# Half 2's best-entry tiles: from diagonal products on TensorE to sums on VectorE, ScalarE and GpSimd; low-part products at the end of a weight

## The chip, the cores and the metric

The kernel runs on one core of a Trainium2 chip. The metric is the device time of one execution in microseconds (us), and of several executions the median. The core has five engines that work through queues of their own, in order, and wait for each other by semaphores: TensorE (in the profile PE, its weight loads PEld), VectorE (DVE), ScalarE (ACT), GpSimd (POOL) and SyncE (SP). DMAs are issued from the queues of SP, ACT and POOL, and 16 DMA engines carry them.

## What is computed

One layer of a decoder on 1024 tokens of width 1024, in float32. First a mixer: a gated linear attention and a chunked gated MLP side by side, merged and projected. Then an expert mixer (PEER), which is where most of the change lies. A token has 8 heads; each head picks its 16 best of 16384 single-neuron experts by two half keys, and the layer sums the experts' outputs:

```python
def peer(h, w_q, keys1, keys2, expert_down, expert_up):
    q = jnp.einsum('btd,dq->btq', h, w_q).reshape(B, T, H, 2, PEER_DQ // 2)
    s1 = jnp.einsum('bthc,kc->bthk', q[..., 0, :], keys1)
    s2 = jnp.einsum('bthc,kc->bthk', q[..., 1, :], keys2)
    v1, i1 = lax.top_k(s1, K)
    v2, i2 = lax.top_k(s2, K)
    ...
    top_s, pos = lax.top_k(cand, K)
    idx = jnp.take_along_axis(cidx, pos, axis=-1)
    g = jax.nn.softmax(top_s, axis=-1)
    def block(args):
        xx, ii, gg = args
        u = expert_down[ii]
        a = jax.nn.gelu(jnp.einsum('pd,ped->pe', xx, u), approximate=False)
        vv = expert_up[ii]
        return jnp.einsum('pe,ped->pd', gg * a, vv)
```

The inputs are drawn so that the scores are far apart: a head's best expert nearly always carries weight, and of the others only a few do. The kernel uses that. Each token's best expert of each head is a "direct entry"; the others, where their gate isn't negligible, are packed into dense lists ("sorted entries"), and a few heads that need more are redone as "rare" rows.

## The kernel before

**Halves and blocks.** The tokens are worked in two halves of 512 (variable `hf`), each of four blocks of 128 tokens: blocks 0 to 3 are half 1, blocks 4 to 7 half 2 (`BH` is 4, the first block of half 2).

**Weight streams.** All large products go through `stream` (L1145): for each of 8 steps k it loads a 128x512 piece of a weight (`wt`, from SP's queue), ACT rounds it to the high part `wh` (L1156), and POOL or DVE takes the rest as the low part `wl` (L1158). `body` then issues for each of four PSUM tiles three products, high by high, high by low and low by high, in `mm3` (L178; products at L179, L180 and L181). `feat` tells the feature-major groups (the weight is stationary: q and k, and the query weights) from the token-major ones (the weight is moving); in the first, `lh` and `ll` are the weight's parts, in the second `rh` and `rl`. So the low part of the weight is used in the third product at L181 of feature-major groups and in the second at L180 of token-major ones. `group` (L1165) is a stream of one weight, `w_out_part` (L1450) one of two, and `w_q` (L1485) is the query projection, whose first weight is streamed in two half-width passes with a body of its own, the other three through `group`. Four buffers each hold `wt`, `wh` and `wl`.

**The expert work beside it.** After each step k, `step` (L945) pumps side queues, generators that emit a little work each time. `direct_rows` (L675) does the direct entries of half 1 while half 2's mixer runs: it gathers an expert's two rows for 128 tokens, forms the dot product on DVE and adds the weighted row to a tile `yd` in SBUF, mostly with DVE (L715), for head 4 with ACT (L712) and POOL (L713). `peer_stream` (L721) does everything else, starting behind half 2's linear attention and going on beyond the last weight. Its list `todo` holds pairs (block, j): j from 0 to 7 are direct entries, one per head, j from 8 to 17 the sorted entries, and 18 (`last`) adds the rare rows and finishes the block. While weights are still streamed, its entries use small buffers (`pl["own"]` is False) and 0.84 to 1.3 pumps a step; behind the last weight it gets its own buffers and a second accumulator (`own` True), and all engines. Entries are listed 2 ahead in the first case (their gathers are issued from POOL's queue, L487), 7 ahead in the second. Each entry takes two pumps.

**A direct entry of half 2.** `direct_list` gathers `uv` (128 tokens by 2048: the expert's input row and its output row, 1 MB); `direct_dot` forms the dot product with `h2l` on DVE (L497), the GELU and the gate on ACT (L499, L500), and a diagonal matrix `Wd` of the weights, also on ACT (L502). `add_rows` (L560) lets PE multiply `Wd` with the output row into the accumulator `acc` in PSUM (L564; two products of 512 columns, in float32). When a run of entries ends, `rows_keep` (L604) copies `acc` to a tile `yb` in SBUF (`kept[b]`, ACT, L609), or adds it to the one that is there (DVE, L606). `rare_rows` (L577) later multiplies `yb` with the modulation row (POOL, L589) and adds it to the block's residual (L590).

**The order.** `EARLY` and `LATER` list the runs of half 2's direct entries. Before the end of the weights (`stage1`) come: 6 rare entries of half 1, blocks 0 to 3, then (5, heads 0 to 3), (6, 0 to 3), (7, 0 to 5) and block 4's heads 0 to 5, whose accumulator stays open. Then come (5, 4 to 7), (6, 4 to 7), (7, 6 and 7), block 4's last two heads with its ten sorted entries, six rare entries, and the rest of blocks 5 to 7. `load_h2` (L460) loads `h2l` once a run, from ACT's queue. Where the weights end before the list up to `stage1` is through, the rest of it is done behind them. The order in which an engine's queue finally holds its instructions is chosen by a planner that places the program's instructions by their order and by durations of its own (`schedule_with_timeline_sim`, L1631), so an instruction can stand ahead of others that the program names first.

## Time and profile before

| | us |
|---|---|
| median of 3 runs (1611.24 to 1613.67) | 1613.54 |
| the profiled execution | 1611.35 |
| its span, from the first instruction to the last | 1609.3 |
| PE / DVE / POOL / ACT busy in it | 1421.2 / 1093.7 / 833.4 / 772.6 |
| POOL: low parts of weights, 257 of 368 | 374.1 |
| DVE: low parts of weights, 111 of 368 | 105.0 |
| ACT: high parts of weights, 368 | 227.2 |
| sorted entries: expert products on PE in the second stage (184 records) | 91.0 |

The profile is one execution as the hardware profiler saw it. A row of a group reads: line, engine, operation, out<-in, shapes, count | busy time in us, mean duration in ns | idle time of the engine just before, and what ended it. One float32 product of the direct entries shows as two records. A busy PE isn't a PE at its peak, since products overlap: one of 128x512 with rounded operands lasts 0.39 us and the next starts 0.23 us behind it. The rows that the argument needs are in the prediction.

### The profile page before, as it was taken

The numbers are of one execution on the slowest core, as the hardware profiler recorded it, in microseconds if no ns is written. First come the engines' busy times: TensorE is split into PE (matmuls) and PEld (weight loads), VectorE is DVE, ScalarE is ACT, GpSimd is POOL, SyncE is SP. The second block draws the span as 40 slices with busy tenths as digits, with TensorE's granted clock in tenths as the row PEclk, the third lists the DMA queues.
The fourth block names the chain that finished last, engine by engine and source line by source line (L and its number), as shares of the span: only waits on it lengthen the run. The fifth ranks groups of instructions, "written<-read, shape, count | busy, mean of one in ns | idle before, by whom it ended". The sixth has DMA issues, their size and how long they took to land.

```text
span 1609.3 us, 20188 instructions
## 1 busy us (share of the span) xinstructions
PE 1421.2 (88%) x6076; PEld 1067.0 (66%) x6076; DVE 1093.7 (68%) x2777; ACT 772.6 (48%) x1677; POOL 833.4 (52%) x682
## 2 busy tenths in 40 slices
PE   5999989999998998898988889998879997778984
PEld 3777757888777786576766667876658764345542
DVE  7664654111446698977788787878787875787782
ACT  4554333332446454745445566556555553445541
POOL 5331247643275455645666688555666563434331
PEclk7999989999999999899999999999999999989998
DMA  9643633224377556737856787956777778978972
GB/s 318 231 143 112 190 125 112 92 85 137 100 247 255 173 167 219 271 99 249 293 181 206 258 302 262 367 190 209 274 268 263 251 275 316 368 293 316 393 292 83
DMA packets 123335, 361.48 MB, mean 225 GB/s; under 512 B 16761, under 2 KB 27257, under 8 KB 107346
## 3 DMA queue, kind: packets, MB, share of 16 engines
q0 software_dynamic: 30336, 175.39, 29.4%
q1 hardware_dynamic: 70272, 132.15, 25.0%
q10 hardware_dynamic: 22610, 52.58, 9.3%
q8 instruction: 49, 0.80, 0.2%
q14 instruction: 68, 0.56, 0.1%
HBM read 335.22 MB, written 24.85 MB: 224 GB/s over the span
## 4 chain that ended last, share of the span: by engine, by line
PE 47%; DVE 21%; DMA 14%; issue 7%; ACT 6%; POOL 4%; ACTq 0%; SPq 0%; DVEq 0%; POOLq 0%
PE mm L180 10%; PE mm L181 10%; PE mm L179 10%; PE acc L564 7%; DMA wada<-in_w_ada_dram 3%; DMA uv<-in_tab_dram,ix 3%; DVE vl L573 2%; DMA uv<-in_tab_dram,dix 2%; DVE uv L542 2%; PE hps L540 2%; DVE wl L1158 1%; DMA uvd<-in_up_dram,dix 1%; PE hps L541 1%; DMA uvd<-in_down_dram,dix 1%; POOL wl L1158 1%
## 5 line engine op out<-in xcount | busy, mean ns | idle before, releaser
L1158 POOL TENSOR_TENSOR wl<-wt,wh 128x512 fp32r<-128x512 f32 x257 | 374.1, 1461 | 355.8 <-ACT wh L1156 320.3
L180 PE MATMUL mm<-wl,hTh 128*128 128x512 f32 x896 | 367.4, 410 | 10.0 <-DVE wl L1158 5.1
L179 PE MATMUL mm<-wh,hTh 128*128 128x512 f32 x896 | 342.7, 412 | 27.2 <-ACT wh L1156 7.7
L1156 ACT ACTIVATE wh<-wt 128x512 fp32r<-128x512 f32 x368 | 227.2, 626 | 281.4 <-PE mm L181 163.8
L181 PE MATMUL mm<-wh,hTl 128*128 128x512 f32 x896 | 361.2, 406 | 0.2 <-DVE hTl L1115 0.2
L179 PEld LDWEIGHTS mm<-wh,hTh 128*128 128x128 f32 x896 | 173.1, 194 | 79.0 <-ACT wh L1156 12.2
L1158 DVE TENSOR_TENSOR wl<-wt,wh 128x512 fp32r<-128x512 f32 x111 | 105.0, 946 | 159.8 <-ACT wh L1156 155.4
L180 PEld LDWEIGHTS mm<-wl,hTh 128*128 128x128 f32 x896 | 173.6, 194 | 56.8 <-POOL wl L1158 9.2
L181 PEld LDWEIGHTS mm<-wh,hTl 128*128 128x128 f32 x896 | 173.4, 194 | 41.7 <-issue 1.3
L179 PE MATMUL mm<-hTh,wh 128*128 128x512 f32 (+1 forms) x448 | 168.1, 377 | 10.5 <-ACT vt L1203 5.3
L487 POOL DMA_INDIRECT uv<-in_tab_dram,ix x92 | 98.5, 1070 | 150.5 <-PE tps L511 35.2
L180 PE MATMUL mm<-hTl,wh 128*128 128x512 f32 (+1 forms) x448 | 164.3, 368 | 0.0
L181 PE MATMUL mm<-hTh,wl 128*128 128x512 f32 (+1 forms) x448 | 159.8, 370 | 1.3 <-DVE wl L1158 0.9
L542 DVE SCALAR_TENSOR_TENSOR uv<-uv,hps 128x512 f32<-128x512 f32 x144 | 95.0, 682 | 38.3 <-PE hps L541 21.0
L573 DVE SCALAR_TENSOR_TENSOR vl<-uv,r,vh 128x512 fp32r<-128x512 f32 x92 | 89.1, 999 | 37.9 <-ACT vh L572 37.9
L179 PEld LDWEIGHTS mm<-hTh,wh 128*128 128x128 f32 x448 | 86.1, 193 | 26.9 <-ACT vt L1203 7.7
L181 PEld LDWEIGHTS mm<-hTh,wl 128*128 128x128 f32 x448 | 85.3, 192 | 16.3 <-DVE wl L1158 1.5
L180 PEld LDWEIGHTS mm<-hTl,wh 128*128 128x128 f32 x448 | 86.2, 192 | 14.0 <-issue 0.7
L564 PE MATMUL acc<-uv,W 128*128 128x512 f32 x184 | 91.0, 618 | 1.4 <-ACT W L557 1.2
L564 PE MATMUL acc<-uv,Wd 128*128 128x512 f32 x128 | 66.0, 655 | 28.1 <-ACT Wd L502 24.3
L540 PE MATMUL hps<-hh,E 128*128 128x512 f32 x144 | 72.3, 508 | 14.4 <-DVE uv L542 7.1
L564 PEld LDWEIGHTS acc<-uv,Wd 128*128 128x128 f32 x128 | 24.9, 206 | 58.4 <-ACT Wd L502 33.6
(958 smaller groups left out, 2662.3 us busy)
## 6 DMA issues: line engine op xcount, KB each, us to landing
wt<-in_w_inp_dram SPq DMA_DIRECT2D x224, 256.0 KB, 3.0
wt<-in_w_qp_dram SPq DMA_DIRECT2D x80, 256.0 KB, 3.2
wada<-in_w_ada_dram SPq DMA_DIRECT2D x32, 512.0 KB, 4.5
wt<-in_w_outp_dram SPq DMA_DIRECT2D x64, 256.0 KB, 3.1
wada<-in_w_ada_dram SPq DMA_DIRECT2D x32, 256.0 KB, 6.0
s_d<-so ACTq DMA_DIRECT2D x32, 256.0 KB, 3.2
h2l<-h_d ACTq DMA_DIRECT2D x13, 512.0 KB, 7.3
xr<-in_x_dram ACTq DMA_DIRECT2D x8, 512.0 KB, 4.1
```

The source lines that it names most:

```text
L179: nc.tensor.matmul(ps, lh, rh, start=first, stop=False)
L180: nc.tensor.matmul(ps, lh, rl, start=False, stop=False)
L181: return nc.tensor.matmul(ps, ll, rh, start=False, stop=last).ins
L487: nc.gpsimd.indirect_dma_start(out=uv[:], out_offset=None, in_=tab, in_offset=bass.IndirectOffsetOnAxis(ap=ix, axis=0))
L540: nc.tensor.matmul(hps, Ej, hh[:, sl], start=True, stop=False)
L541: nc.tensor.matmul(hps, Ej, hl[:, sl], start=False, stop=True)
L542: nc.vector.scalar_tensor_tensor(uv[:, sl], uv[:, sl], 1.0, hps, op0=OP.mult, op1=OP.mult, accum_out=r[:, 2 + n:3 + n])
L564: nc.tensor.matmul(acc[:, sl], W, v[:, sl], start=first, stop=last)
L573: nc.vector.scalar_tensor_tensor(vl, v, r[:, 5:6], vh.bitcast(F32), op0=OP.mult, op1=OP.subtract)
L1156: nc.scalar.activation(wh, wt, AF.Identity)
L1158: eng.tensor_tensor(wl, wt, wh.bitcast(F32), op=OP.subtract)
```

## The change

Two things are changed.

1. `mm3s` replaces the calls of `mm3` in `group` and in `w_out_part`. In steps 1 to 6 of a stream it issues, for all four PSUM tiles, the two products that don't need the weight's low part, and then the four that do. In steps 0 and 7 the order is the old one. Query weight 0, with its two half-width passes, keeps `mm3`.

2. The direct entries of half 2 are no longer multiplied by a diagonal on PE. `direct_dot` gives the weight column and the output row to `direct_sum`: the first entry of a block creates `kept[b]` on ACT, the others are added to it, with `own` and an even head by DVE in one operation, else by ACT (scaling the row in place) and POOL (the add). `rows_keep` is left with the add. A run of direct entries opens no accumulator. The lists change: heads 4 and 5 of blocks 5 and 6 come in the first list in the place of block 4's heads 0 to 5, and block 4's eight heads are the last run of the second list, just ahead of its sorted entries.

```diff
-EARLY = ((5, 0, 4), (6, 0, 4), (7, 0, 6))
-LATER = ((5, 4, 8), (6, 4, 8), (7, 6, 8))
+EARLY = ((5, 0, 4), (6, 0, 4), (7, 0, 6), (5, 4, 6), (6, 4, 6))
+LATER = ((5, 6, 8), (6, 6, 8), (7, 6, 8), (4, 0, 8))
...
+    def mm3s(sets, k):
+        if k in (0, KD - 1):
+            for ps, lh, ll, rh, rl, feat in sets:
+                mm3(ps, lh, ll, rh, rl, k == 0, k == KD - 1)
+            return
+        for ps, lh, ll, rh, rl, feat in sets:
+            nc.tensor.matmul(ps, lh, rh, start=False, stop=False)
+            nc.tensor.matmul(ps, *((lh, rl) if feat else (ll, rh)), start=False, stop=False)
+        for ps, lh, ll, rh, rl, feat in sets:
+            nc.tensor.matmul(ps, *((ll, rh) if feat else (lh, rl)), start=False, stop=False)
...
-        W = pl["pq"].tile([P, P], F32, name="Wd", tag="W", bufs=3 if pl["own"] else 2)
-        nc.scalar.activation(W, ident, AF.Identity, scale=r[:, 2:3])
-        yield W, uv[:, D:]
+        yield r[:, 2:3], uv[:, D:]
+
+    def direct_sum(pl, b, j, wv):
+        w, v = wv
+        if b not in kept:
+            kept[b] = rowp.tile([P, D], F32, name="yb", tag="row") if b > BH else pl["ph"].tile([P, D], F32, name="yb")
+            nc.scalar.activation(kept[b], v, AF.Identity, scale=w)
+        elif pl["own"] and j % 2 == 0:
+            nc.vector.scalar_tensor_tensor(kept[b], v, w, kept[b], op0=OP.mult, op1=OP.add)
+        else:
+            nc.scalar.activation(v, v, AF.Identity, scale=w)
+            nc.gpsimd.tensor_tensor(kept[b], kept[b], v, op=OP.add)
...
     def rows_keep(pl, b, acc):
-        if b in kept:
-            nc.vector.tensor_tensor(kept[b], kept[b], acc, op=OP.add)
-            return
-        kept[b] = rowp.tile([P, D], F32, name="yb", tag="row") if b > BH else pl["ph"].tile([P, D], F32, name="yb")
-        nc.scalar.activation(kept[b], acc, AF.Identity)
+        nc.vector.tensor_tensor(kept[b], kept[b], acc, op=OP.add)
...
+        def direct(b, j0, j1):
+            runs.add((b, j0))
+            todo.extend((b, j) for j in range(j0, j1))
+
         rows = range(PH, last + 1)
         seg(NBLK, range(PH, PH + NTR[0]))
         for b in range(BH):
-            seg(b, range(0 if b not in summed else PH, last + 1))
-        for b, j0, j1 in EARLY:
-            seg(b, range(j0, j1))
-        seg(BH, range(6), close=False)
+            seg(b, rows)
+        for run_ in EARLY:
+            direct(*run_)
         stage1 = len(todo)
-        for b, j0, j1 in LATER:
-            seg(b, range(j0, j1))
-        seg(BH, range(6, last), open_=False)
+        for run_ in LATER:
+            direct(*run_)
+        seg(BH, range(PH, last))
...
             nw = weights(nw, nd)
+            if j < PH:
+                direct_sum(use[-1], b, j, wvs.pop(k))
+                del ents[k]
+                yield
+                continue
...
-                    for i in range(4):
-                        cs = slice(i * P, (i + 1) * P)
-                        if feat:
-                            mm3(pss[i], wh[:, cs], wl[:, cs], hTh[:, k], hTl[:, k], k == 0, k == KD - 1)
-                        else:
-                            mm3(pss[i], hTh[:, k, cs], hTl[:, k, cs], wh, wl, k == 0, k == KD - 1)
+                    cuts = [slice(i * P, (i + 1) * P) for i in range(4)]
+                    if feat:
+                        mm3s([(pss[i], wh[:, cs], wl[:, cs], hTh[:, k], hTl[:, k], True) for i, cs in enumerate(cuts)], k)
+                    else:
+                        mm3s([(pss[i], hTh[:, k, cs], hTl[:, k, cs], wh, wl, False) for i, cs in enumerate(cuts)], k)
...
-                    for m in range(4):
-                        cs = slice((2 * p + m // 2) * P, (2 * p + m // 2 + 1) * P)
-                        mm3(pss[m], hTh[:, k, cs], hTl[:, k, cs], ws[m % 2][0], ws[m % 2][1], k == 0, k == KD - 1)
+                    cuts = [slice((2 * p + m // 2) * P, (2 * p + m // 2 + 1) * P) for m in range(4)]
+                    mm3s([(pss[m], hTh[:, k, cs], hTl[:, k, cs], *ws[m % 2], False) for m, cs in enumerate(cuts)], k)
```

More of the change, by code (lines that the diff above doesn't have):

```diff
@@ L727, in seg @@
                 opens.add((b, js[0]))
-            if js[0] < PH:
-                runs.add((b, js[0]))
             todo.extend((b, j) for j in js)
```

## The prediction

> **What bounds the kernel now.** I read the page first (span, engines, chain), then the windows that cut the span where the direct entries of half 2 run, then the groups and the waits of those windows, and the timeline last.
>
> ```profile
> span 1609.3 us, 20188 instructions
> PE 1421.2 (88%) x6076; PEld 1067.0 (66%) x6076; DVE 1093.7 (68%) x2777; ACT 772.6 (48%) x1677; POOL 833.4 (52%) x682
> PE 47%; DVE 21%; DMA 14%; issue 7%; ACT 6%; POOL 4%; ACTq 0%; SPq 0%; DVEq 0%; POOLq 0%
> PE mm L180 10%; PE mm L181 10%; PE mm L179 10%; PE acc L564 7%; DMA wada<-in_w_ada_dram 3%; DMA uv<-in_tab_dram,ix 3%; DVE vl L573 2%; DMA uv<-in_tab_dram,dix 2%; DVE uv L542 2%; PE hps L540 2%; DVE wl L1158 1%; DMA uvd<-in_up_dram,dix 1%; PE hps L541 1%; DMA uvd<-in_down_dram,dix 1%; POOL wl L1158 1%
> ```
>
> TensorE holds most of the chain: the weight products L179 to L181 and, with 7%, the expert sums of L564. The direct entries touch only two stretches, so I cut the span there.
>
> ```profile
> core 0: us, PE busy (x) PEld busy (x) DVE busy (x) ACT busy (x) POOL busy (x), PEclk, DMA share, GB/s
> 0.00:1270.00 1270.00, 1148.79 (x5180) 907.40 (x5181) 855.87 (x1840) 622.30 (x1247) 699.97 (x563) 0.96 0.61 207
> 1270.00:1347.00 77.00, 72.68 (x309) 52.95 (x307) 53.22 (x221) 36.45 (x78) 43.20 (x40) 0.98 0.78 277
> 1347.00:1420.00 73.00, 48.12 (x116) 21.30 (x117) 56.27 (x216) 31.06 (x92) 30.51 (x27) 0.88 0.81 308
> 1420.00:1609.30 189.30, 151.65 (x474) 85.36 (x472) 128.35 (x502) 82.82 (x262) 59.76 (x55) 0.91 0.73 287
> ```
>
> From 1270 to 1347 (**stage A**, the last query weights with direct entries between them) PE is busy 72.7 of 77 us: it is the bound. From 1347 to 1420 (**stage B**, direct entries and the routing of half 2, no weights left) no engine fills the time: DVE has 56.3, the DMA engines 81%, PE 48. That stage is a chain through all of them. Behind 1420 no direct entry is left.
>
> ```profile
> L564 PE MATMUL acc<-uv,Wd 128*128 128x512 f32 x128 | 66.0, 655 | 28.1 <-ACT Wd L502 24.3 <-DVE yb L606 2.2 <-issue 1.4
> L564 PE MATMUL acc<-uv,Wd 128*128 128x512 f32 x40 | 19.8, 622 | 2.8 <-ACT Wd L502 2.8
> L564 PE MATMUL acc<-uv,Wd 128*128 128x512 f32 x85 | 45.0, 672 | 25.3 <-ACT Wd L502 21.5 <-DVE yb L606 2.2 <-issue 1.4
> ```
>
> These are the diagonal products: whole run, stage A, stage B (three records more lie on the edge). 128 records for 32 entries are four each, so 10 entries fall in stage A and 22 in stage B. The number of steps that an entry takes does not change, so I keep that split.
>
> **Part 1, low-part products last.** What it can win is the time that PE waits for a wl:
>
> ```profile
> PE mm L180 <- DVE wl L1158: 5.1, 2, 4.0
> PE mm L180 <- POOL wl L1158: 4.6, 7, 1.3
> PE mm L181 <- DVE wl L1158: 0.9, 1, 0.9
> PE mm L181 <- POOL wl L1158: 0.5, 1, 0.5
> ```
>
> That is 11.1 us in all, the ceiling. The first product with wl moves from second place (third in the feature-major groups) to ninth. The pace is the distance of two starts:
>
> ```profile
> 1275.73 0.39 PE L180 MATMUL mm<-hTl,wh 128*128 128x512 f32 x1
> 1275.96 0.39 PE L181 MATMUL mm<-hTh,wl 128*128 128x512 f32 x1
> ```
>
> 0.23 us, so a late wl gains 7 x 0.23 = 1.6 us. Of the wait of 4.0 us 1.6 go, of the other at L180 from DVE 1.1, of the seven from POOL all 4.6: 7.3. Steps 0 and 7 of a stream keep the old order; with 6 of 8 steps that is 5.5, and I take **-6**. No product is added; wh is free four products earlier. Bounds: 0 (a wh that is late instead) and -11.
>
> **Part 2, the sums leave PE.** The 32 entries become 4 that create kept[b] on ACT (the first of each block), 10 that DVE adds (even heads among the 22 of stage B), and 18 that ACT scales and POOL adds: 3 + 0 + 7 in stage A, 1 + 10 + 11 in stage B. Half 1 already does the same operations on the same shapes, and those rows give the prices:
>
> ```profile
> L715 DVE SCALAR_TENSOR_TENSOR yd<-uvd,rdr,yd 128x1024 f32<-128x1024 f32 x24 | 32.8, 1365 | 4.3 <-DMA uvd<-in_up_dram,dix 4.0
> L502 ACT ACTIVATE Wd<-ident,rd 128x128 f32<-128x128 f32 x32 | 12.8, 401 | 7.6 <-PE acc L564 6.5 <-ACT rd L500 0.4
> L713 POOL TENSOR_TENSOR yd<-yd,uvd 128x1024 f32<-128x1024 f32 x4 | 11.2, 2798 | 10.7 <-ACT uvd L712 10.7
> L708 ACT ACTIVATE yd<-uvd,rdr 128x1024 f32<-128x1024 f32 x4 | 4.6, 1149 | 1.3 <-DVE rdr L706 1.3
> L712 ACT ACTIVATE uvd<-uvd,rdr 128x1024 f32<-128x1024 f32 x4 | 4.6, 1142 | 4.1 <-DVE rdr L706 2.8 <-DMA uvd<-in_up_dram,dix 1.3
> L609 ACT ACTIVATE yb<-acc 128x1024 f32<-128x1024 f32 x4 | 4.1, 1020 | 2.9 <-PE acc L564 2.9
> L606 DVE TENSOR_TENSOR yb<-yb,acc 128x1024 f32<-128x1024 f32 x3 | 3.7, 1218 | 4.2 <-PE acc L564 4.2
> ```
>
> ACT loses 32 diagonals and four copies of an accumulator (12.8 + 4.1) and gains 18 x 1.14 and 4 x 1.15 (25.1 together): 8 us more on an engine that is busy 48% and waits in both stages, so I cost it at nothing. If it came late, the POOL add behind it would wait (rival D).
>
> Stage A. PE loses 19.8 us of products and the wait of 2.8: 22.6, down to 54.4. Who is late next?
>
> ```profile
> L487 POOL DMA_INDIRECT uv<-in_tab_dram,dix x16 | 17.6, 1100 | 18.0 <-PE mm L181 5.1 <-PE acc L564 4.9 <-PE aux L1537 3.7
> L1158 POOL TENSOR_TENSOR wl<-wt,wh 128x512 fp32r<-128x512 f32 x12 | 16.8, 1404 | 15.6 <-ACT wh L1156 11.6 <-DMA wt<-in_w_qp_dram 3.9
> L646 POOL TENSOR_TENSOR fin<-fin,fw 128x1024 f32<-128x1024 f32 x1 | 2.4, 2412 | 0.0
> L497 DVE SCALAR_TENSOR_TENSOR uv<-uv,h2l 128x1024 f32<-128x1024 f32 x11 | 16.0, 1453 | 16.1 <-DMA uv<-in_tab_dram,dix 13.9 <-issue 2.2
> L366 DVE COPY_PREDICATED v<-bits,v 128x448 f32<-128x448 uint32 (+3 forms) x8 | 9.3, 1163 | 0.0
> ```
>
> POOL has 43.2 us there (gathers, low parts, three steps of 2.4 like L646 for a finished block). Seven adds of 2.80 make 62.8: the stage cannot be shorter than that, a gain of 14. And POOL and DVE shut each other out:
>
> ```profile
> 1393.39 2.40 POOL L589 TENSOR_TENSOR yb<-yb,g2row 128x1024 f32<-128x1024 f32 x1 [0.22 <-DVE yb L606]
> 1404.80 3.26 POOL L589 TENSOR_TENSOR yb<-yb,g2row 128x1024 f32<-128x1024 f32 x1 [5.88 <-DVE yb L606]
> 1393.50 2.31 DVE L398 TENSOR_TENSOR qr<-qt,lane 128x1 f32<-128x1 f32 x1
> 1404.63 1.22 DVE L497 SCALAR_TENSOR_TENSOR uv<-uv,h2l 128x1024 f32<-128x1024 f32 x1
> ```
>
> An operation of DVE on one column took 2.31 us and ended with POOL's multiply, which had started just before it; POOL's next one started behind a DVE product and took 0.86 longer. If such pairs exclude each other wholly, stage A needs 16.0 + 9.3 (DVE) + 16.8 + 3 x 2.4 + 7 x 2.8 (POOL) = 68.9, a gain of 8. Between 8 and 14 I take **-10**; ends 0 and -22.6. The Trainium skill has this as a rule that speaks against the change: by "SBUF — State Buffer", section "Who interferes with whom", a VectorE instruction with two SBUF inputs and a GpSimd instruction that reads SBUF share one port pair, and the second blocks until the first has ended. By that rule, with which the four rows above agree, the gain is the 8 and not the 22.6.
>
> Stage B.
>
> ```profile
> L497 DVE SCALAR_TENSOR_TENSOR uv<-uv,h2l 128x1024 f32<-128x1024 f32 x21 | 25.1, 1215 | 4.7 <-DMA uv<-in_tab_dram,dix 4.7
> L589 POOL TENSOR_TENSOR yb<-yb,g2row 128x1024 f32<-128x1024 f32 x3 | 8.0, 2672 | 7.2 <-DVE yb L606 7.2
> POOL uv L487 <- PE acc L564: 9.8, 5, 5.0
> ```
>
> What goes: PE's 45.0 us, POOL's wait of 9.8 for gather buffers that PE frees, DVE's wait of 4.2 (L606) and its three adds of 3.7. What comes: DVE 10 x 1.37 = 13.7, so 66.3 of 73 in its queue; POOL 11 x 2.80 = 30.8, so 61.3. The DMA engines need 0.81 x 73 = 59 for the same rows. Without mutual blocking DVE's 66.3 would be the floor: -7. With it, 25.1 + 13.7 + 30.8 + 8.0 = 77.6: +5. The rows show the blocking, so I take **+4**. The first gather of block 4's sorted entries waits on the routing that is threaded through this DVE queue, so what the stage loses delays all that follows.
>
> Moved steps: block 4's entries leave stage A's list and four of blocks 5 and 6 take their place, with their gathers on POOL; the runs of one block become nine in place of eight, so one load of h2 more goes into ACT's queue.
>
> ```profile
> h2l<-h_d ACTq DMA_DIRECT2D x13, 512.0 KB, 7.3
> ```
>
> It is hidden while the seven entries gathered ahead are worked off; without that cover it costs 7.3. Two accumulators are free in stage B where block 4 held one, but nothing of that stage accumulates any more: nothing.
>
> **Sum.** -6 - 10 + 4 = -12. The profiled execution took 1611.35 us (span 1609.3 and 2 around it), so 1599.4; it lies 2.2 under the median of 1613.54, which becomes 1601.5.
>
> **Rivals.**
> - B, **all hides**: DVE, POOL and ACT overlap as they do in most of the span (68%, 52%, 48% busy) and PE's relief comes through: -8 - 20 - 7 = -35, 1578.5. For it: PE is the bound in stage A and most POOL idle time there was a wait on others. Against: the blocking rows.
> - C, **blocking takes it back**: POOL adds of 3.26, as in the row at 1404.80, make 72.1 in stage A (-5) and 82.7 in stage B (+10): -6 - 5 + 10 = -1, 1612.5. For it: those rows; against: half of DVE's work there (top-k, PSUM reads) need not collide. It is what the Trainium skill's rule above ("SBUF — State Buffer") would make of the time.
> - D, **POOL waits in its queue**: an add waits for the row that ACT scales, and behind it stand the gathers and low parts. L713 shows POOL idle 10.7 us before four adds, 2.7 each. In stage A 7 x (2.8 + 2.7) + 43.2 = 81.7 (+5), in stage B 11 x 5.5 + 30.5 = 91 (+18): 17 more with part 1, 1630.5. It decides from a wait of 1.1 us an add in stage B (30.5 + 11 x 3.9 = 73). Against: in half 1 an add had little else to follow; here the dot product runs an entry ahead.
> - That the reordering does nothing, because the wait moves to wh, is the zero end of part 1; it shifts every case by 6.
>
> **How the numbers follow.** A, the sum: 0.50 (own range 1592 to 1611). B 0.18, C 0.14, D 0.18. I forecast A, 1601.5. The range runs from 1577, inside B, to 1622, between C and D, which leaves about a tenth on each side. About 0.2% (3 us) is what a measurement can tell from no change: A and B are faster (0.68), C is the same (0.12 with the ends of its neighbours), the rest, D and a bad C, is slower (0.20).
>
> **What would show it.** Part 1: the waits for wl at L180 and L181 fall from 11.1 to about 5 and those for wh do not grow by it. Stage A: from the start of the third query group to the last key product some 10 us less, PE no longer at 94%, POOL's busy share over 85%. Stage B: as long as now or longer, with DVE near 90% busy, DVE operations on few columns that take over 2 us, POOL adds of 2.4 to 3.3. B is right if adds stay at 2.4 and stage B falls under 68 us; D if POOL idles over 1 us before an add for ACT. The sum is wrong from the start if the planner of the issue order places other work differently before 1270, where only part 1 acts.

## The result and the profile after

The changed kernel takes 1629.05 us, the median of 4 runs (1625.36 to 1636.17), beside 1612.79 for the kernel before, also of 4. The medians lie 16 us apart; the ratio taken from all these runs is 1.0107, 95% interval 1.0071 to 1.0144, which is 17 us. It is slower, where 12 us less were forecast. The profiled execution took 1627.85 us. From its page, engines and chain:

```profile
PE 1365.9 (84%) x5948; PEld 1048.7 (64%) x5948; DVE 1151.2 (71%) x2784; ACT 788.8 (49%) x1669; POOL 880.4 (54%) x701
DVE 18%; PE 17%; ACT 5%; issue 5%; DMA 4%; POOL 1%; ACTq 0%; SPq 0%; DVEq 0%; POOLq 0%
```

PE lost 55 us of work (1421.2 before), DVE gained 58 and POOL 47. The chain does not reach back over the whole span, so these shares aren't comparable with those of before one by one; but DVE now leads it.

To see where the time went I cut both spans at two events that both kernels have: the start of the last weight product, and the start of the first dot product of a sorted entry of half 2 (DVE, uv<-uv,hps). Windows of after, then of before; the columns are the window, its length, busy time of PE, PEld, DVE, ACT and POOL with counts, granted clock, DMA share, GB/s:

```profile
1270.00:1322.90 52.90, 43.58 (x198) 35.67 (x196) 40.76 (x175) 24.65 (x46) 42.20 (x31) 0.90 0.67 230
1322.90:1447.20 124.30, 16.57 (x65) 12.89 (x63) 117.79 (x338) 55.50 (x125) 76.74 (x56) 0.54 0.74 267
1447.20:1626.10 178.90, 145.25 (x454) 80.57 (x454) 123.54 (x420) 74.50 (x239) 60.71 (x53) 0.92 0.75 287
```

```profile
1270.00:1339.80 69.80, 66.99 (x284) 49.42 (x283) 50.75 (x217) 33.82 (x69) 38.64 (x36) 0.98 0.77 273
1339.80:1425.60 85.80, 57.31 (x157) 27.07 (x155) 62.98 (x257) 37.60 (x110) 38.54 (x33) 0.90 0.82 311
1425.60:1609.30 183.70, 148.15 (x458) 83.11 (x458) 124.11 (x465) 78.91 (x252) 56.28 (x51) 0.91 0.72 285
```

The weights end 16.9 us earlier, as meant. The sorted entries take 4.8 us less. But the stretch between, with the direct entries that come behind the weights, grew from 85.8 to 124.3 us: +38.5. (Below, "the stretch" is this one.) PE is nearly idle there, at half its clock, and DVE is busy 117.8 of 124.3 us, where it had 63.0 of 85.8. The groups of the stretch in the changed kernel:

```profile
L508 DVE SCALAR_TENSOR_TENSOR uv<-uv,h2l 128x1024 f32<-128x1024 f32 x25 | 34.4, 1406 | 1.0 <-DMA uv<-in_tab_dram,dix 1.0
L523 POOL TENSOR_TENSOR yb<-yb,uv 128x1024 f32<-128x1024 f32 x13 | 31.8, 2442 | 19.2 <-DVE yb L520 10.1 <-ACT uv L522 8.3 <-DVE tsq L207 0.5
L520 DVE SCALAR_TENSOR_TENSOR yb<-uv,rd,yb 128x1024 f32<-128x1024 f32 x8 | 12.0, 1497 | 0.3 <-ACT rd L511 0.3
L359 DVE TENSOR_TENSOR g<-dd,sm 128x8 f32<-128x8 f32 x2 | 4.9, 2463 | 0.0
L283 DVE TENSOR_TENSOR end<-start,cnt 128x1 f32<-128x1 f32 x1 | 3.0, 3039 | 0.0
L388 DVE TENSOR_TENSOR_SCAN qinc<-ones,flags 128x32 f32<-128x32 f32 x1 | 3.0, 3021 | 0.0
```

An operation on one column of 128 tokens took 3.04 us, one on eight columns 2.46. The timeline of DVE and POOL shows why (start, duration, engine, line):

```profile
1345.22 2.34 POOL L523 TENSOR_TENSOR yb<-yb,uv 128x1024 f32<-128x1024 f32 x1 [3.09 <-ACT uv L522]
1345.25 0.29 DVE L204 FIND_INDEX8 ti<-tv,so 128x8 uint32<-128x128 f32 x1
...
1354.70 2.63 DVE L359 TENSOR_TENSOR g<-dd,sm 128x8 f32<-128x8 f32 x1
1354.94 2.35 POOL L523 TENSOR_TENSOR yb<-yb,uv 128x1024 f32<-128x1024 f32 x1
...
1357.95 3.02 DVE L388 TENSOR_TENSOR_SCAN qinc<-ones,flags 128x32 f32<-128x32 f32 x1
1358.53 2.34 POOL L523 TENSOR_TENSOR yb<-yb,uv 128x1024 f32<-128x1024 f32 x1
```

An operation of DVE that meets an add of POOL waits for its end, and DVE's queue stands behind it: the short ones shown end with the add. Each of the 13 adds met such an operation. Not all operations meet it: the index search at 1345.25 took its usual 0.29 us inside an add, and of the operations that search for maxima and their places (MAX8, FIND_INDEX8, MATCH_VALUE_LOAD) 143 started inside a POOL operation of over 1 us in this profile, and none was stretched by 0.2 us. To measure the blocking, I took each operation of DVE in the stretch and compared its duration with the shortest of the same line and shape in that profile; a difference over 0.2 us is put to the POOL operation that overlaps it longest. That makes 39.3 us of **blocked DVE time** in the changed kernel, 30.0 of them beside its 13 adds, 2.3 us an add. In the kernel before it is 3.1 us. Operations that DVE does itself for a sum are cheaper: one multiply-add is 1.37 us in half 1 (L715 in the prediction).

### The profile page after: what moved, and what is told of

It reads as the page before. It is cut to its first block, busy times and chain, and to the rows that moved or that the text cites. A ratio compares the mean times of both kernels' runs of the same rounds, so it can differ in the third digit from the quotient of the medians.

```text
span 1626.1 us, 19949 instructions
## 1 busy us (share of the span) xinstructions
PE 1365.9 (84%) x5948; PEld 1048.7 (64%) x5948; DVE 1151.2 (71%) x2784; ACT 788.8 (49%) x1669; POOL 880.4 (54%) x701
## 4 chain that ended last, share of the span: by engine, by line
DVE 18%; PE 17%; ACT 5%; issue 5%; DMA 4%; POOL 1%; ACTq 0%; SPq 0%; DVEq 0%; POOLq 0%
PE acc L584 4%; PE mm L185 2%; PE mm L184 2%; DVE uv L508 2%; PE mm L187 2%; DVE uv L562 1%; PE hps L560 1%; DVE E L684 1%; PE hps L561 1%; DVE wl L1180 1%; DVE jk L536 1%; DVE vl L593 1%; DMA s_d<-so 1%; PE mm L190 1%; PE mm L191 1%
## 5 line engine op out<-in xcount | busy, mean ns | idle before, releaser
L184 PE MATMUL mm<-wh,hTh 128*128 128x512 f32 x672 | 274.8, 411 | 4.0 <-ACT wh L1178 3.9
L187 PE MATMUL mm<-wl,hTh 128*128 128x512 f32 x672 | 213.4, 405 | 5.9 <-DVE wl L1180 4.6
L184 PEld LDWEIGHTS mm<-wh,hTh 128*128 128x128 f32 x672 | 130.9, 195 | 38.7 <-ACT wh L1178 7.4
L187 PEld LDWEIGHTS mm<-wl,hTh 128*128 128x128 f32 x672 | 128.2, 193 | 40.6 <-DVE wl L1180 6.7
L185 PEld LDWEIGHTS mm<-wh,hTl 128*128 128x128 f32 x672 | 131.1, 195 | 32.3 <-issue 1.6
L190 PE MATMUL mm<-wh,hTh 128*128 128x512 f32 x224 | 92.5, 426 | 18.8 <-DVE sg L1385 7.1
L184 PE MATMUL mm<-hTh,wh 128*128 128x512 f32 x240 | 96.0, 400 | 0.0
L185 PE MATMUL mm<-hTl,wh 128*128 128x512 f32 x240 | 95.8, 399 | 0.0
L191 PE MATMUL mm<-wl,hTh 128*128 128x512 f32 x224 | 92.0, 411 | 3.9 <-POOL wl L1180 3.6
L190 PE MATMUL mm<-hTh,wh 128*128 128x256 f32 (+1 forms) x208 | 71.2, 346 | 7.5 <-ACT vt L1224 5.0
L192 PE MATMUL mm<-hTh,wl 128*128 128x256 f32 (+1 forms) x208 | 68.9, 340 | 3.6 <-DVE wl L1180 2.2
L191 PE MATMUL mm<-hTl,wh 128*128 128x256 f32 (+1 forms) x208 | 70.4, 340 | 1.7 <-DVE hTl L176 1.7
```

Of the source, the lines that this page charges most:

```text
L184: nc.tensor.matmul(ps, lh, rh, start=False, stop=False)
L185: nc.tensor.matmul(ps, *((lh, rl) if feat else (ll, rh)), start=False, stop=False)
L187: nc.tensor.matmul(ps, *((ll, rh) if feat else (lh, rl)), start=False, stop=False)
L190: nc.tensor.matmul(ps, lh, rh, start=first, stop=False)
L191: nc.tensor.matmul(ps, lh, rl, start=False, stop=False)
L192: return nc.tensor.matmul(ps, ll, rh, start=False, stop=last).ins
```

## The experiments

All kernels were timed against the kernel before, in the same way as the changed one, and each ratio is to the runs of the kernel before that were made beside it (medians from 1612.8 to 1617.6 us). "Weights" is the start of the last weight product, "rest" goes from the first sorted dot product to the end; both, the stretch and the blocked time are from one profile, in us, whose time can lie some us off the median.

| run | ratio and 95% interval | weights | stretch | rest | DVE blocked |
|---|---|---|---|---|---|
| before | 1 | 1339.8 | 85.8 | 183.7 | 3.1 |
| changed | 1.0107 [1.0071, 1.0144] | 1322.9 | 124.3 | 179.0 | 39.3 |
| e1 reordering alone | 0.9949 [0.9930, 0.9967] | 1337.8 | 86.0 | 182.4 | 3.1 |
| e2 diagonals behind the weights | 0.9998 [0.9980, 1.0016] | 1328.9 | 106.2 | 179.4 | 20.0 |
| e3 PE kept warm | 1.0120 [1.0092, 1.0148] | 1321.0 | 125.7 | 179.8 | 38.5 |
| e4 sums behind the weights on DVE | 1.0008 [0.9989, 1.0027] | 1328.6 | 106.3 | 182.7 | 16.5 |
| e5 new order, diagonals | 1.0017 [0.9995, 1.0038] | 1340.6 | 94.2 | 185.9 | 2.0 |
| e6 no sums behind the weights | 0.9958 [0.9940, 0.9976] | 1325.9 | 101.3 | 177.4 | 14.1 |
| e7 POOL without reads | 0.9991 [0.9973, 1.0010] | 1321.5 | 107.4 | 179.0 | 28.3 |
| e8 eight sums beside, POOL | 0.9941 [0.9910, 0.9972] | 1329.6 | 98.2 | 177.2 | 4.9 |
| e9 seven runs, diagonals | 0.9997 [0.9978, 1.0016] | 1334.2 | 90.3 | 186.6 | 5.5 |
| e10 seven runs, sums | 1.0084 [1.0057, 1.0111] | 1322.7 | 122.2 | 178.3 | 33.7 |
| e11 e8 with seven runs | 0.9956 [0.9937, 0.9976] | 1325.9 | 96.1 | 185.5 | 11.2 |
| e12 part 2 without part 1 | 1.0163 [1.0132, 1.0194] | 1337.4 | 124.9 | 182.3 | 36.7 |
| e13 e8 with a third score row | 0.9941 [0.9919, 0.9962] | 1315.5 | 104.1 | 173.2 | 9.6 |
| e14 e1 with a third score row | 0.9983 [0.9958, 1.0007] | 1341.6 | 87.9 | 184.6 | 3.6 |
| e15 eight sums beside, DVE | 0.9880 [0.9844, 0.9916] | 1326.9 | 88.1 | 177.9 | 7.7 |
| e16 all sums on DVE | 0.9977 [0.9956, 0.9997] | 1322.8 | 93.5 | 190.7 | 5.5 |
| e17 fourteen sums, DVE | 0.9944 [0.9919, 0.9970] | 1326.1 | 99.1 | 178.1 | 7.6 |

### The parts, the clock and the engine that adds

**e1.** The kernel before with `mm3s` in `group` and `w_out_part`, nothing else.

> The kernel before with the low-part products last and nothing else. In the two profiles product 3840 of the weights starts 10.2 us earlier in the changed kernel, ahead of any direct entry of half 2. If that is the reordering's own gain, this kernel takes 10 us less than before, about 1602.5, with the stretch from the last weight product to the first gather of block 4's sorted entries as before (79 us) and 191 us from there to the end. If the reordering upsets the later stages or costs clock, 1610 to 1630.

Measured: 0.9949, 8.2 us of 1616. Part 1 is a gain. Its waits for the parts of weights, whole run:

```profile
PE mm L184 <- ACT wh L1167: 6.0, 6, 1.8
PE mm L187 <- DVE wl L1169: 5.4, 4, 3.0
PE mm L191 <- POOL wl L1169: 3.6, 2, 2.4
PE mm L192 <- DVE wl L1169: 2.2, 1, 2.2
PE mm L190 <- ACT wh L1167: 1.9, 3, 1.1
PE mm L192 <- POOL wl L1169: 1.2, 2, 0.8
PE mm L187 <- POOL wl L1169: 1.1, 2, 0.8
PE mm L191 <- DVE wl L1169: 0.3, 1, 0.3
```

The waits for wl sum to 13.8 us, against 11.1 before, and those for wh to 7.9, against 7.7. So their sum, from which the gain was reckoned, did not fall. In the profiles most of the gain lies early: the products from number 384 to 576 of 4032 take 71.8 us in place of 78.8. There the largest of the waits shrank, first in the kernel before, then in e1:

```profile
223.55 0.79 PE L180 MATMUL mm<-wl,hTh 128*128 128x512 f32 x1 [4.00 <-DVE wl L1158]
221.24 1.20 PE L187 MATMUL mm<-wl,hTh 128*128 128x512 f32 x4 [0.33 <-DVE wl L1169]
```

Behind this wait the next products start 0.43 us apart in the kernel before, 0.23 in e1. The wait fell by 3.7 us, where 1.6 were reckoned; DVE makes that low part behind the last operation of L1354 in the kernel before, and ahead of the last three of them in e1. In e12, which has the old order, it is 4.8 us, in the other runs with part 1 from 0.3 to 2.5. Other waits for wl came in its place.

**e2.** The changed kernel, but a direct entry that comes behind the weights goes through the diagonal again.

```diff
+        if not pl["own"]:
+            yield r[:, 2:3], uv[:, D:]
+            return
+        W = pl["pq"].tile([P, P], F32, name="Wd", tag="W", bufs=3)
+        nc.scalar.activation(W, ident, AF.Identity, scale=r[:, 2:3])
+        yield W, uv[:, D:]
```

> The changed kernel, but the direct entries listed behind the weights (22 of 32) go back to diagonal products on PE and an accumulator; those beside the weights keep ACT and POOL. Theory: what was lost is lost behind the weights, through DVE shut out by POOL's adds (stage B, 22 us) and through the low TensorE clock that follows an idle PE (11 us). Then this takes 1613 - 17 = 1596, stage B 79 us, the rest 191 us. Rival: the adds beside the weights leave a debt on DVE and POOL that is paid behind them in any case; then stage B stays near 100 us and the time near 1620.

Measured: 0.9998. Of the changed kernel's 1.07% over before, 1.09 go with the sums behind the weights. But the stretch is still 106.2 us, 20 more than with the reordering alone and near what the rival expected, although no entry listed behind the weights is summed in SBUF. Its blocked time is 20.0 us, 12.4 of them beside adds that were listed beside the weights and came late.

**e3.** The changed kernel with two products a direct entry behind the weights whose result is read by nobody, to keep PE's clock up.

```diff
+        if pl["own"]:
+            for n in range(2):
+                hps = pl["hp"].tile([P, 512], F32, name="hps")
+                nc.tensor.matmul(hps, ident, us[n], start=True, stop=True)
```

> The changed kernel with two idle products on PE per direct entry behind the weights (identity by the used-up half of the gathered tile, into a PSUM tile that nobody reads), as many as the diagonal took. Clock theory: the granted clock stays near 0.9 between 1340 and 1453 in place of 0.5, and the stretch of sorted entries (first gather of block 4 to the end, 202 us) falls back to 191; stage B keeps its 101 us; 1618. Rival, DVE and POOL alone: the stretch stays at 202 us, as its extra time is adds that were left over; 1629.

Its window of the stretch:

```profile
1321.00:1446.70 125.70, 61.48 (x147) 30.74 (x145) 116.20 (x328) 55.16 (x124) 77.13 (x54) 0.69 0.74 263
```

PE does 61.5 us and its clock is 0.69 in place of 0.54, yet nothing gets shorter: 1.0120. The clock did not reach the 0.9 that was expected, so this run alone settles it only in part; but e4, next, keeps the clock of 0.54 and loses nothing. The low clock is a companion of the idle PE, not the cause.

**e4.** The changed kernel with DVE doing all sums behind the weights.

```diff
-        elif pl["own"] and j % 2 == 0:
+        elif pl["own"]:
```

> The changed kernel with all sums behind the weights on DVE, none on POOL: 11 more operations of 1.28 us on DVE (14 us), 11 adds fewer on POOL. Exclusion theory: DVE loses some 28 us in stage B to operations that stretch beside POOL's adds (32 us over their shortest, against 3 before); without these stage B falls from 101 to about 87, and the whole to 1615, the clock still low. Rival, DVE's own added work makes the length: stage B grows by 14 to 115, 1643. Rival, POOL waits in its queue: stage B falls by POOL's waits for ACT and DVE of about 14, too, but DVE's short operations stay stretched.

```profile
1328.60:1435.00 106.40, 17.68 (x65) 13.61 (x63) 99.74 (x309) 41.00 (x106) 55.57 (x45) 0.54 0.85 310
```

DVE gets more to do and is busy 18 us less (99.7 against 117.8). The ratio is 1.0008. That DVE's own share of the sums were the price is thereby refuted; the adds on POOL are, with the scaling on ACT that goes with each.

### The order, the floor, and what an add reads

**e5.** Part 1 and the changed kernel's order, every entry through a diagonal (in e2's edit the condition is dropped).

> The kernel before with part 1 and with the changed kernel's new order of the direct entries (block 4 last, nine runs), every sum still a diagonal product on TensorE; it computes the same. It asks whether the order itself costs time. If the loss comes from the sums (theory: VectorE and GpSimd exclude each other), the order is free: ratio to the kernel before 0.993 to 0.998, like the reordering alone (0.9949), and 86 to 90 us from the last weight product to the first dot product of a sorted entry of half 2. If the order or the extra load of h2 costs it (rival), 1.000 or more and 95 to 106 us in that stretch, as where the diagonals came back behind the weights (106.2).

Measured: 1.0017, so the order by itself costs 0.7% with diagonals (11 us, e1 to e5), and the stretch is 94.2: the rival's case, if by a little less. Two rows of e5's timeline, with the idle time ahead of the instruction and what ended it in brackets:

```profile
1384.68 0.32 ACTq L474 DMA_DIRECT2D h2l<-h_d  x1
...
1407.41 1.23 DVE L508 SCALAR_TENSOR_TENSOR uv<-uv,h2l 128x1024 f32<-128x1024 f32 x1 [11.95 <-DMA h2l<-h_d]
```

The h2 row of block 7's last run is asked for at 1384.7, and the dot product that needs it starts 22.7 us later; DVE stands idle for 11.9 of them.

**e6.** The changed kernel; behind the weights the additions are left out, with the scaling ahead of them; the creations stay.

```diff
-        elif pl["own"] and j % 2 == 0:
+        elif pl["own"]:
+            pass
+        elif False:
```

> The changed kernel with every addition behind the weights left out but those that create an accumulator (it leaves out the weighted rows of those entries; gathers, dot products and gates stay). It is the floor for the stretch behind the weights when the sums cost nothing there. If the sums are the whole loss: 82 to 92 us from the last weight product to the first sorted dot product (changed kernel 124.3, before 85.8), ratio 0.985 to 0.992. If what the sums beside the weights leave behind (entries that come later, adds in GpSimd's queue) accounts for the 20 us that were left with diagonals behind the weights, the stretch stays at 100 to 108 and the ratio at 0.997 to 1.002.

Measured: 0.9958, stretch 101.3 us. The sums behind the weights are 23 of the 38.5 us. Even without them 15 remain, with four adds in the stretch that were listed beside the weights and came late.

**e7.** Each add of POOL behind the weights becomes two memsets of the row.

```diff
-            nc.gpsimd.tensor_tensor(kept[b], kept[b], v, op=OP.add)
+            if pl["own"]:
+                nc.gpsimd.memset(v, 0.0)
+                nc.gpsimd.memset(v, 0.0)
+            else:
+                nc.gpsimd.tensor_tensor(kept[b], kept[b], v, op=OP.add)
```

> The changed kernel with each GpSimd add behind the weights replaced by two memsets of the row (they leave out those sums): the same place in GpSimd's queue and the same wait for ScalarE, but no SBUF input. If the exclusion of VectorE by adds that read SBUF is the cause, VectorE's operations are stretched by under 12 us in that stretch (31.8 in the changed kernel) and it takes 95 to 108 us instead of 124. If GpSimd's occupied queue and its waits are the cause (gathers late behind adds), it stays at 115 to 125 as long as two memsets take over 2 us. If a memset takes much less than 1.2 us, the run does not tell the two apart.

Its groups and its timeline:

```profile
L524 POOL MEMSET uv<- 128x1024 f32 x10 | 9.6, 961 | 8.6 <-ACT uv L522 8.6
L525 POOL MEMSET uv<- 128x1024 f32 x9 | 8.6, 961 | 0.2
```

```profile
1357.69 1.49 DVE L303 TENSOR_SCALAR wk<-tsel 128x224 f32<-128x224 f32 x1
1358.07 0.98 POOL L525 MEMSET uv<- 128x1024 f32 x1
```

A pair of memsets lasts 1.92 us against 2.44 of an add, and waits for ACT as the add did (8.6 us over the pairs; in the changed kernel 8.3 over the 13 adds). The stretch falls to 107.4 and the ratio to 0.9991: 17 of the 23 us go. So the wait for ACT in POOL's queue is not what those 17 us are. The run does not part all of POOL's queue from the blocking: a pair is under the 2 us that the expectation asked for, ten pairs take 5 us less of POOL than ten adds, and a memset does not read `yb`, so that POOL's wait of 10.1 us for DVE's multiply-adds is gone too. My figure for the blocked time (under 12 us) was missed, with 28.3: 17.2 stand beside adds listed ahead and the modulation products of L613, 10.2 beside memsets, though these read nothing. What they stretch are operations such as the one shown, 1.49 us where it takes 0.26 in the changed kernel; dot products and multiply-adds beside memsets kept their 1.2 to 1.3 us. The Trainium skill, "SBUF — State Buffer", section "Who interferes with whom", says that a GpSimd instruction that only writes leaves VectorE instructions with two SBUF inputs alone, but shuts out copies and tensor-scalar operations in their two-port modes; the trace agrees, as far as it shows (which mode an operation ran in, it does not).

**e8.** Part 1 and the old order; the first eight entries (blocks 5 and 6, heads 0 to 3) are summed by ACT and POOL, all others by diagonals.

```diff
+SUMS = [(b, j) for b in (5, 6) for j in range(4)]
...
+            if (b, j) in SUMS:
+                direct_sum(b, wvs.pop(k))
+                del ents[k]
+                yield
+                continue
```

> The kernel before with part 1 and its own order of entries; only the first eight direct entries of half 2 (four each of blocks 5 and 6, which run beside the weights) are summed in SBUF by ScalarE and GpSimd, all others by diagonal products. It computes the same. If GpSimd has room for six adds beside the weights, the last weight product starts 6 to 9 us earlier than with the reordering alone and the stretch behind it stays at 86 to 90 us: ratio 0.989 to 0.993. If every GpSimd add there is paid back by gathers and entries that come later, the stretch behind grows by what was gained: 0.994 to 1.000.

Measured: 0.9941, no better than the reordering alone. The weights end 8.2 us earlier than in e1, and the stretch is 12.2 longer: the second expectation. The adds from 1270 to the last weight product, in e8 and in the changed kernel:

```profile
L527 POOL TENSOR_TENSOR yb<-yb,uv 128x1024 f32<-128x1024 f32 x4 | 9.6, 2399 | 11.4 <-ACT uv L526 11.4
L523 POOL TENSOR_TENSOR yb<-yb,uv 128x1024 f32<-128x1024 f32 x4 | 9.6, 2404 | 11.0 <-ACT uv L522 10.9
```

POOL stands 2.9 and 2.7 us before each add for the row that ACT scales, and the gathers stand behind it. When the weights end, seven dot products are done in e8 and in the changed kernel, nine in e1 and before.

### Runs of entries

**e9, e10, e11.** Block 4's eight entries in one run at the end, seven runs in all; with diagonals (e9), with the changed kernel's sums (e10), and with e8's eight sums (e11).

```diff
+EARLY = ((5, 0, 4), (6, 0, 4), (7, 0, 6))
+LATER = ((5, 4, 8), (6, 4, 8), (7, 6, 8), (4, 0, 8))
```

> The kernel before with part 1 and every sum a diagonal product, but in an order of seven runs: blocks 5, 6, 7 as before, and all eight entries of block 4 in one run at the end (the changed kernel has nine runs, three of them of two entries; before has eight). It computes the same. If the order of the changed kernel costs time by its short runs, whose h2 rows arrive late (VectorE stood idle 11.9 us for one in the run before), this one is as fast as the reordering alone: ratio 0.991 to 0.996, 82 to 88 us from the last weight product to the first sorted dot product. If it costs time because block 4 comes last, 0.999 to 1.003 and 92 to 98 us.

> The changed kernel, sums and all, with the seven runs in place of its nine. It computes the same. If the late h2 rows add to the loss beside the sums, it gains what the order cost with diagonals: ratio 1.003 to 1.007 and 112 to 119 us behind the last weight product (changed kernel 1.0107 and 124.3). If VectorE, which is busy all the time there, hides those loads, the order costs nothing in the changed kernel: 1.009 to 1.013 and 121 to 127 us.

> Part 1, the first eight direct entries of half 2 summed by ScalarE and GpSimd beside the weights, all others by diagonals, in the seven runs. It computes the same. It asks whether the time that the weights win (8 us with the eight sums) reaches the end once the order has the fewest loads. If the stretch behind the weights is bound by VectorE's own queue (9.2 to 9.9 of 10 us from 1350 to 1410 in the eight-sum run), it does not: 0.992 to 0.996, like the eight sums or the reordering alone. If the loads of h2 were in its way, 0.987 to 0.991.

Measured: e9 0.9997, so short runs aren't the point (its stretch, 90.3, lies between the two expected). Two rows of its timeline, and a window between them:

```profile
1377.13 0.32 ACTq L474 DMA_DIRECT2D h2l<-h_d  x1
...
1398.90 1.23 DVE L508 SCALAR_TENSOR_TENSOR uv<-uv,h2l 128x1024 f32<-128x1024 f32 x1 [14.60 <-DMA h2l<-h_d]
```

```profile
1380.00:1390.00 10.00, 6.15 (x10) 2.01 (x8) 3.51 (x5) 1.80 (x6) 7.81 (x6) 0.83 1.03 417
```

Here it is the load for block 4 that is asked for at 1377.1 and used 21.8 us later, with DVE idle for 14.6 of them and the DMA engines full (1.03 from 1380 to 1390): it shares them with the gathers that were issued ahead. In e5 the engines were as full (1.01 from the load to its use). That these late loads are what the order costs is not shown by a run of its own. The reordering alone shows no wait of DVE for h2 in its stretch. With the sums (e10) seven runs in place of nine are worth 2 us of the stretch, and the intervals of e10 and the changed kernel overlap. No wait of DVE for h2 shows in the changed kernel's stretch: where DVE is busy all the time, the load comes late for nobody. The sums in the old order were not run. e11 is e8 again.

**e12.** The changed kernel with all products in the old order.

> The changed kernel without part 1: products in the old order. It computes the same. If the gain of part 1 (ratio 0.9949 by itself) comes through in the changed kernel too, this is slower by as much: 1.014 to 1.018. If the stretch behind the weights gives it back, because VectorE's and GpSimd's work there waits for nothing that the weights hold up, 1.008 to 1.012.

Measured: 1.0163. Part 1 is worth 0.56% in the changed kernel as well, though the intervals of e12 and the changed kernel touch; as far as that goes, the two parts add up.

### What the weights win

**e13, e14.** A third buffer for the score rows (`so` and the tiles that share its buffers), and one buffer fewer for a scratch row (`jk`), in e8 and in e1.

```diff
-                so = rp.tile([P, 512], F32, name="so", bufs=2)
+                so = rp.tile([P, 512], F32, name="so", bufs=3)
```

> The run with eight sums beside the weights (ratio 0.9941), with three buffers in place of two for the score rows (so) that ScalarE copies and a DMA stores, and one scratch row fewer to make room. It computes the same. In the eight-sum run ScalarE waited 6.7 us for the store of a score row to leave its buffer while the gathers filled the DMA engines, and VectorE waited 9.1 us for the next score row behind it. If that wait is what takes back the 8 us won beside the weights, it falls to under 3 us, the stretch behind the last weight product shortens from 98.2 to 88 to 93 us, and the ratio is 0.988 to 0.992. If DMA or VectorE is the bound there anyhow, the stretch stays at 96 to 100 us and the ratio at 0.993 to 0.996.

> The control: the same third score buffer in the kernel with the reordering alone (ratio 0.9949), where no wait for a store shows behind the weights. It computes the same. Both theories: 0.993 to 0.997, 84 to 88 us behind the last weight product.

Measured: 0.9941 and 0.9983. The wait for the store fell only from 6.7 to 4.0 us and the stretch did not shorten, so nothing speaks for it as what takes the gain back. The control missed its expectation: e14 is 0.3% behind e1, with intervals that touch. If the edit itself costs that, e13 hides a gain as large, and the two runs do not exclude it. (The profiled execution of e13 took 1594.5 us, 11 under its median, and was 14 us ahead of e8's before 1270 already; so its "weights" and "rest" say less than its ratio.)

**e15.** e8 with DVE in the place of ACT and POOL.

```diff
-            nc.scalar.activation(v, v, AF.Identity, scale=w)
-            nc.gpsimd.tensor_tensor(kept[b], kept[b], v, op=OP.add)
+            nc.vector.scalar_tensor_tensor(kept[b], v, w, kept[b], op0=OP.mult, op1=OP.add)
```

> Part 1 and the eight sums beside the weights, as in the eight-sum run, but six of them as multiply-adds of VectorE (two create the accumulator on ScalarE), with no add on GpSimd. It computes the same. If the adds on GpSimd (six of 2.4 us, with gathers and low parts behind them) slow the entries beside the weights, this one has more dot products done when the weights end (nine, as with diagonals, against seven) and ends earlier: 0.987 to 0.992. If what is won beside the weights is taken back by the stores and gathers behind them, 0.993 to 0.996 as with GpSimd.

```profile
1326.90:1415.10 88.20, 62.31 (x161) 29.13 (x160) 79.67 (x347) 44.92 (x131) 48.50 (x44) 0.85 0.98 387
```

Measured: 0.9880, 1594.99 us, the fastest kernel of the study. The weights end 10.9 us earlier than in e1 and the stretch is 2 longer. What took the gain back in e8 were the adds of POOL with the scaling of ACT, which this run replaces together (the intervals of e8 and e15 overlap by a hair, 0.9910 to 0.9916). (Not nine dot products are done when the weights end, as I expected, but eight; that end is 10.9 us earlier, though, and the ninth and the eleventh start at 1328.2 and 1344.2, in e8 at 1340.7 and 1356.8.)

**e16.** The changed kernel with all 28 additions on DVE. **e17.** e15 with the fourteen entries of the first list.

> The changed kernel, its order and both parts, with every one of its 28 additions on VectorE as a multiply-add and none on GpSimd (before: ten on VectorE). It computes the same. If the adds on GpSimd are the whole loss beyond the order, this one is no slower than diagonals in the same order (1.0017) and gains beside the weights what eight sums on VectorE gained: 0.992 to 0.999. If VectorE's own queue behind the weights is the bound, the 22 multiply-adds there cost as much as they did with GpSimd's adds beside the weights: 0.999 to 1.003.

> The best run so far (eight sums on VectorE beside the weights, 0.988) with the multiply-adds for all fourteen entries of blocks 5, 6 and 7 that are listed beside the weights (eleven adds, three creations); it computes the same. Five of those entries come to their sum behind the weights, where VectorE is the fuller engine and TensorE has room: if that queue is the bound, 0.988 to 0.993, no better than eight. If TensorE's diagonals still hold the entries up there, 0.984 to 0.987.

Two groups of the stretch in e16:

```profile
L520 DVE SCALAR_TENSOR_TENSOR yb<-uv,rd,yb 128x1024 f32<-128x1024 f32 x18 | 22.6, 1275 | 0.6 <-ACT rd L511 0.6
L508 DVE SCALAR_TENSOR_TENSOR uv<-uv,h2l 128x1024 f32<-128x1024 f32 x24 | 30.5, 1302 | 3.7 <-DMA uv<-in_tab_dram,dix 3.0 <-issue 0.7
```

Measured: e16 0.9977, the stretch 93.5 us with 18 multiply-adds of DVE, beside 124.3 with eight of DVE and 13 adds of POOL. Moving POOL's adds, and ACT's scaling, to DVE takes 1.3% from the changed kernel. Its sorted part takes 190.7 us in place of 179.0; from 1410 to 1460 POOL's gathers wait 24.7 us for their indices (ACT ix), and I did not follow that further. e17 is 0.9944, above both ranges expected: five more adds on DVE, all of them behind the weights, give back what the eight had won over the reordering alone. There DVE is the fuller engine, and PE has room for diagonals.

## Why the prediction was wrong

One ladder leads from before to the changed kernel, each step one edit, in ratios (0.1% is 1.6 us): reordering 0.9949, with the new order 1.0017, with the sums beside the weights 0.9998, with the sums behind them 1.0107. That is -8, +11, -3 and +18 us; the -3 lies within the intervals. The shares hang on the sequence: the 11 us of the order are those with diagonals, and what the order costs with the sums in place no run shows. Against the ladder, the steps of the prediction:

- **What bounds the kernel**: right for stage A. For stage B it was said that no engine fills the time. True of before; the change filled DVE.
- **Part 1, -6**: right in sign and nearly in size (-8 in e1, -9 from e12 to the changed kernel). The mechanism came true for the largest wait for a wl, which fell from 4.0 to 0.3 us, but others came, and their sum rose from 11.1 to 13.8 where it should have fallen to about 5.
- **Stage A, -10**: the weights did end that much earlier (8.2 in e8, 11.7 from e5 to e2, 10.9 in e15). What failed is that it was counted as a gain at the end. With POOL's adds it comes back in the stretch (+12.2 in e8, +12.0 from e5 to e2): the entries fell behind (the split of entries between the stages was kept as it was, but seven dot products and not nine were done when the weights ended), and POOL stood 2.7 us before each add. That is the very price that rival D took from L713; that ACT's work costs nothing was wrong for the same reason. How much is the wait and how much the add itself, no run parts. With DVE's multiply-adds the gain arrives (e15).
- **Moved steps, nothing**: wrong where there is room to see it, +11 us with diagonals (e5 against e1). The load of h2 was held to be covered by the seven entries gathered ahead. Those gathers are no cover but the traffic it has to share the DMA engines with, and in place of 7.3 us it took 22.7 and 21.8 from its issue to its first use in e5 and e9 (that this makes the 11 us is argued from those waits, not tested). In the changed kernel itself DVE waited for no h2.
- **Stage B, +4: this is the step that failed most.** It measured +18 (e2 to the changed kernel; 23 us of stretch against e6). The mechanism, that POOL and DVE shut each other out, was seen and named from two rows; the sum was made with DVE's dot products and multiply-adds only, 25.1 + 13.7 + 30.8 + 8.0 = 77.6. But a short operation of DVE that meets an add stands as long as a large one, and the queue with it, so all of DVE's work belongs into that floor: its 56.3 us of the window (less the three adds of 3.7 that go) + 13.7 + 30.8 + 8.0 - 3.1 that is blocked already = 102 us, 29 over the 73 of before; less the searches, 13 us of that window, which need not wait, it is 89, or 16 over. Bar the 3.1 and the 13, this sum could have been made from the rows shown. Measured, it holds: in the stretch of the changed kernel DVE has 117.8 - 39.3 = 78.5 us of its own and POOL 40.6 of adds and products of over 1.5 us, together 119 of 124.3. "Half of DVE's work there need not collide" was true of some operations (the searches above) and of little use: the 13 adds found operations that did, for 30.0 us in all.
- **Two accumulators, nothing**: no run separates it.
- **Rivals.** C named the mechanism and sized it by POOL's adds, at 3.26 us; they took 2.44, and it is DVE that pays, 2.3 us an add. D gave 1630.5, close to the result, by POOL's wait for ACT. Beside the weights the wait is there (2.7 us an add) and goes with what took the gain. Behind them it is 0.6 us an add (8.3 over 13), under the 1.1 from which D decides; 10.1 more of POOL's 19.2 is a wait for DVE's multiply-adds. e7, which keeps the wait for ACT, shows it to be the lesser part. So that D's number was met is luck: behind the weights it was met mostly by C's mechanism.
- **What would show it**: adds of 2.4 us, DVE near 90% and short operations over 2 us all came; read together, they mean a stretch longer by the adds, which the sum left out. POOL's share in stage A over 85% did not come (42.2 of 52.9 us, 80%), nor did the fall of the waits for wl.

Not tried: the sums on DVE for exactly those entries that come to their sum before the last weight; the order with block 4's h2 loaded before the gathers.

## What to carry to other kernels

Two engines that shut each other out are one engine for the sum: add the whole queue of the one, its smallest operations too, to the durations of the other. A sum handed to GpSimd cost VectorE 2.3 us of standing still, where doing it itself costs 1.3; here it paid neither behind the weights (e4 and e16 against the changed kernel) nor beside them (e15 against e8). And time that the bound of a stage wins counts only if the queues that feed the next stage (here gathers behind adds) don't fall behind by as much.

## What the hardware showed beyond that

PE's granted clock stood at 0.50 from 1340.9 to 1453.5 us, while PE was nearly idle (15.5 us busy in those 112.6; before, the clock is 0.89 from 1340 to 1420):

```profile
1340.90:1453.50 112.60, 15.51 (x40) 10.30 (x41) 107.50 (x300) 47.36 (x114) 71.82 (x49) 0.50 0.73 263
```

The Trainium skill, "TensorE: Matmul & The Clock Gate", section "Part 1: The HAM clock gate", has the half rate for an idle array, and the trace agrees; but the sorted part behind it took 179.0 us in the changed kernel and 179.8 with PE kept warmer, so that here a half clock cost nothing that could be seen. The other surprise were the loads of 512 KB that took 23 and 22 us to their first use beside gathers that kept the DMA engines full; from the page of the changed kernel, with the median from issue to landing at the end:

```profile
h2l<-h_d ACTq DMA_DIRECT2D x14, 512.0 KB, 6.2
```
